# Where the rows of the output projection are kept, and when they are fetched, in a hybrid decoder layer

## The chip, the core and the metric

The kernel runs on one core of a Trainium2 chip. The core has a matrix engine (PE, with its weight loads shown as PEld), three engines for element-wise work (DVE, ACT, POOL), a queue (SP) from which the DMA transfers are issued, and 16 DMA engines that carry them out. Matmul results go to PSUM, eight banks of 128 partitions by 512 words; everything else that is worked on lies in SBUF. The metric is the device time of one execution in microseconds (us), lower being better.

## What is computed

One decoder layer over 1024 tokens of width 1024, in float32:

```
h = rmsnorm(x, mix_pre_norm);  z = h @ w_in
a = mla(...)                         # latent attention, 8 heads
c = short_gated_conv(...)
m = concat(rmsnorm(a), rmsnorm(c))
x = x + rmsnorm(m @ w_out, mix_post_norm)
h = rmsnorm(x, ffn_pre_norm)
f = (silu(h @ w_gate) * (h @ w_up)) @ w_down
x = x + rmsnorm(f, ffn_post_norm)
e = rmsnorm(p @ w_ple_proj, ple_norm)
return x + sigmoid(x @ w_ple_gate) * e
```

The change lies between the attention and the FFN: in the product with w_out, the residual sum, the norm before the FFN and the turn of its result for the FFN.

## The kernel before

**Precision.** Every float32 operand is split into a high and a low part (`split`, L208 to L215: ACT makes the high part, DVE the low one), and every product is three matmuls (`mm3`, L217 to L223: high x high, high x low, low x high).

**Memory.** SBUF is shared out by hand. The arena `mem_r` holds split operands, `mem_f` float32 values: 30 units of 512 words on each partition. An arena call `mf(n, where)` takes n neighbouring units within the ranges of `where`; of the free ones it takes those that have been free longest, and with n = 2 and a range it steps by 2. "Free" is meant in the order in which the program is written. At run time an instruction that writes a place waits until the earlier readers and writers of that place are done, the DMA transfers among them. PSUM banks are given out in turn by `ps.get`.

**Order.** Each engine, and SP, works through its own list in order. The lists are made from the order of the program text by a scheduler, which may put an instruction ahead of others on the same engine; so the order in a trace isn't always that of the text.

**The stage.** The output projection runs over T = 8 tiles of 128 tokens. Its half over the convolution's channels, `wo_c`, runs early, beside the attention, and leaves its rows in `y_d` in DRAM. The other half runs in the loop at L1261, `for t in range(T + 2)`. For a tile t these steps follow each other, each one turn of the loop or more after the one before:

- `load_y(t)` (L1056) fetches the row y of tile t from y_d, 128 x 1024 words, two units.
- `wo_a(t)` (L1071): 24 matmuls (L221 to L223) into two PSUM banks, then DVE adds them to y (L1074) and so empties the banks; then the mean square on ACT (L231) and its root on POOL (L228).
- `load_x(t)` (L1060) fetches the row of the residual stream; `wo_x1(t)` (L1078) norms y, adds that row (L1080, L1082, on DVE) and stores the sum to x1_d (L1084); then the next mean square.
- `wo_n(t)` (L1089) writes the normed row into the place of the x row (L1092) and frees y.
- `h2_turn(t)` (L1103) transposes that row on PE (L1113), copies it out of PSUM and splits it. For the first four tiles the copy goes to a place `raw` (L1108, L1115), from which it is stored to `hr_d` (L1123). For the last four it goes straight into `tr[0]` and `tr[1]` (L1117), four units each, which become the FFN's blocks B12 and B22.

Turn t of the loop runs wo_a(t), wo_x1(t-1), load_x(t), wo_n(t-2), h2_turn(t-3) and, at its end, load_y(t+1) for t from 1 to 6; load_y(0) and load_y(1) stand ahead of the loop. The rows y, the rows x and raw are taken from the range `ML`, units 0 to 21. Of these the gains g_mix and g_ffn hold 18 to 21 until the end of the loop, and the weights of the FFN's first pair of blocks, raw_load(0, 0), hold four of units 0 to 7. tr[0] holds units 22 to 25 and tr[1] units 26 to 29 from before the loop.

**Behind it.** After the eighth wo_a come the first products of the FFN (`product`, L1199 to L1202), whose weights are fetched by raw_load (L1155); raw_load(1, 0) and raw_load(0, 1) take places in units 0 to 17 at t = 8 and t = 9. The FFN uses a scheme with seven products for eight (p = 1 to 7); the blocks for the others are sums and differences made on DVE (L1315) and split (L210, L211). hr_d is read back at t = 9.

Of the kernel before, what the change touches and what calls it, by code (L numbers as in the profile page):

```python
# [45 lines left out]
T = S // P  # L46
# [53 lines left out]
def free(*bufs):  # L100
    for b in bufs:
        m = b.arena
        m.clock += 1
        for i in range(b.lo, b.lo + b.n):
            assert m.live[i]
            m.live[i] = False
            m.freed[i] = m.clock
# [28 lines left out]
def hybrid_layer(ctx: ExitStack, tc: tile.TileContext, x, x_t, p_t, cols_in, positions,  # L136
# [16 lines left out]
    mf = Arena(big.tile([P, FU * U], F32, name="mem_f"), FU)  # L153
# [19 lines left out]
    RR = ((64, 72), (16, 24))  # L173
    RG = ((56, 72),)
    BJ = ((32, 64),)
    ML, MG, MW = ((0, 22),), ((18, 22),), ((0, 8),)


    zeros = cp.tile([P, U // 2], mybir.dt.bfloat16, name="zeros")
# [27 lines left out]
    def split(h, l, src, gain=None, eng=None):  # L207

        if gain is None:
            act.copy(h, src)  # L210
            (eng or dve).tensor_tensor(l, src, h.bitcast(F32), op=ALU.subtract)  # L211
        else:
            act.mul(h, src, gain)
            dve.scalar_tensor_tensor(l, src, gain, h.bitcast(F32), op0=ALU.mult,
                                     op1=ALU.subtract)  # L215
# [20 lines left out]
    def bank3(ap, k):  # L236
        return ap.rearrange("p (k c) -> p k c", k=k)
# [330 lines left out]
    for step in START.split():  # L568
        op, t = step[0], int(step[1:] or 0)
# [484 lines left out]
    rows_y, rows_x = {}, {}  # L1054

    def load_y(t):  # L1056
        rows_y[t] = mf(2, ML)
        sp.dma_start(rows_y[t].a, y_d[t * P : (t + 1) * P, :])

    def load_x(t):  # L1060
        rows_x[t] = mf(2, ML)
        sp.dma_start(rows_x[t].a, x[t * P : (t + 1) * P, :])

    def row_norm(t, i):
# [6 lines left out]
    def wo_a(t):  # L1071
        y = rows_y[t].a
        ids, b = wo_half(t, mTa, 0)
        dve.scalar_tensor_tensor(y, b, ss_a[:, t : t + 1], y, op0=ALU.mult, op1=ALU.add)  # L1074
        ps.put(ids)
        row_norm(t, 0)

    def wo_x1(t):  # L1078
        y, xr = rows_y[t].a, rows_x.pop(t)
        dve.scalar_tensor_tensor(y, y, ss_y[:, 2 * t : 2 * t + 1], g_mix.a, op0=ALU.mult,  # L1080
                                 op1=ALU.mult)
        dve.tensor_tensor(y, y, xr.a, op=ALU.add)  # L1082
        rows_n[t] = xr
        sp.dma_start(x1_d[t * P : (t + 1) * P, :], y)  # L1084
        row_norm(t, 1)
# [3 lines left out]
    def wo_n(t):  # L1089

        y = rows_y.pop(t)
        dve.scalar_tensor_tensor(rows_n[t].a, y.a, ss_y[:, 2 * t + 1 : 2 * t + 2], g_ffn.a,  # L1092
                                 op0=ALU.mult, op1=ALU.mult)
        free(y)
# [3 lines left out]
    tf, tr = {}, {}  # L1098

    def four(b):  # L1100
        return b.a.rearrange("p (k c) -> p k c", k=4)

    def h2_turn(t):  # L1103
        src = rows_n.pop(t)
        o = slice(t % 4 * P, (t % 4 + 1) * P)
        first = t < T // 2
        if first:
            raw = mf(2, ML)  # L1108
        for q in range(2):
            ids, b = ps.get()  # L1110
            for j in range(4):
                k = 4 * q + j
                pe.transpose(b[:, j * P : (j + 1) * P], src.a[:, k * P : (k + 1) * P], ident[:])  # L1113
            if first:
                act.copy(raw.a[:, q * U : (q + 1) * U], b)  # L1115
            else:
                act.copy(four(tr[q])[:, :, o], bank3(b, 4))  # L1117
            if first or q:
                h, l = tf["B" + "12"[q] + "12"[not first]]
                split(four(h)[:, :, o], four(l)[:, :, o], bank3(b, 4))  # L1120
            ps.put(ids)
        if first:
            sp.dma_start(hr_d[:, :, o], raw.a.rearrange("p (k c) -> p k c", k=KD))  # L1123
            free(raw)
        free(src)
# [12 lines left out]
    def pair(n, where):  # L1138
        return mr(n, where), mr(n, where)
# [11 lines left out]
    def raw_load(fp, i, where=None):  # L1151

        for m, w in enumerate((w_gate, w_up)):
            raws[fp, m, i] = r = mf(2, where)
            sp.dma_start(r.a, w[2 * fp + i])  # L1155

    def factor(fp, m, p):
        eng = pool if fp else dve
        a = raws[fp, m, 0].a
        a11, a12 = a[:, 0:U], a[:, U:]  # L1160
        if p == 1:
            src = a11
        elif p == 2:
            src = a12
        else:
            b = raws[fp, m, 1].a
            a21, a22 = b[:, 0:U], b[:, U:]
            if p == 6:
                eng.tensor_tensor(a21, a21, a22, op=ALU.add)
                eng.tensor_tensor(a11, a21, a11, op=ALU.subtract)  # L1170
                src = a11
            elif p == 5:
                src = a21
            elif p == 7:
                eng.tensor_tensor(a21, a22, a11, op=ALU.subtract)
                src = a21
            elif p == 3:
                eng.tensor_tensor(a12, a12, a11, op=ALU.subtract)
                src = a12
            else:  # L1180
                src = a22
        h, l = wp[fp, m, p] = pair(1, RR)
        split(h.a, l.a, src)
        if p == ORDER[-1]:
            free(raws.pop((fp, m, 0)), raws.pop((fp, m, 1)))
# [3 lines left out]
    def product(fp, m, p):  # L1189
        key = fp, m, {1: "X", 6: "X", 7: "X", 4: "X", 2: "Z", 5: "Y", 3: "Y"}[p]  # L1190
        if key not in bank:
            bank[key] = ps.get()
        ids, b = bank[key]
        wh, wl = wp.pop((fp, m, p))
        th, tl = (four(v) for v in tf[RIGHT[p]])
        first, last = p in (1, 2, 5), p in (2, 3, 4)
        for k in range(4):
            c = slice(k * P, (k + 1) * P)
            pe.matmul(b, wh.a[:, c], th[:, k], start=first and k == 0, stop=False,  # L1199
                      skip_group_check=True)  # L1200
            pe.matmul(b, wh.a[:, c], tl[:, k], start=False, stop=False, skip_group_check=True)  # L1201
            pe.matmul(b, wl.a[:, c], th[:, k], start=False, stop=k == 3, skip_group_check=True)  # L1202
        free(wh, wl)

        c = {1: "11", 2: "11", 6: "12", 3: "12", 5: "22", 7: "22", 4: "21"}[p]
        if p in (1, 6, 5, 4):
            blk[fp, m, c] = mf(1, ((0, 18), (22, 30)) if fp < 3 else None)
        o = blk[fp, m, c].a
        g = blk[fp, 0, c].a
        if p in (1, 6, 5):  # L1210
            act.copy(o, b)
        elif p == 4 and m == 0:
            act.activation(o, b, AF.Silu)
        elif p == 4:
            dve.tensor_tensor(o, b, g, op=ALU.mult)
        else:
            dve.tensor_tensor(o, b, o, op=ALU.add)  # L1217
            if m == 0:
                act.activation(o, o, AF.Silu)
            else:  # L1220
                dve.tensor_tensor(o, o, g, op=ALU.mult)
        if last:
            ps.put(ids)
            del bank[key]
# [30 lines left out]

    load_y(0)
    load_y(1)
    raw_load(0, 0, MW)
    tr[0], tr[1] = mf(4, ((22, 26),)), mf(4, ((26, 30),))
    head = [(0, m, p) for p in (1, 2) for m in range(2)]  # L1260
    for t in range(T + 2):  # L1261
        if t < T:
            wo_a(t)
        elif t == T:
            for d in (mTa, wo):
                for h, l in d.values():
                    free(h, l)
            for i in head[:2]:
                product(*i)
        elif t == T + 1:  # L1270
            for i in head[2:]:
                product(*i)
        if 1 <= t <= T:
            wo_x1(t - 1)
        if t == T:
            free(g_mix)
        if t < T:
            load_x(t)
        if 2 <= t <= T + 1:
            wo_n(t - 2)  # L1280
        if t == T + 1:
            free(g_ffn)
            tf["T1"], tf["T4"] = pair(4, BT), pair(4, BT)
            b11, b21 = tf["T1"][1].a.bitcast(F32), tf["T4"][1].a.bitcast(F32)
            sp.dma_start(b11.rearrange("p (k c) -> p k c", k=4), hr_d[:, 0:4, :])
            sp.dma_start(b21.rearrange("p (k c) -> p k c", k=4), hr_d[:, 4:8, :])
        if t >= 3:
            h2_turn(t - 3)
        if 1 <= t < T - 1:
            load_y(t + 1)  # L1290
        if t == T + 1:
            raw_load(0, 1, ((0, 18),))
        if t == T:
            raw_load(1, 0, ((0, 18),))
            for m in range(2):
                raws[2, m, 0] = r = mr(2, BT)
                r.a = r.a.bitcast(F32)
                sp.dma_start(r.a, g2_d[m])
        if t == T // 2:
            for i in head:  # L1300
                factor(*i)
# [246 lines left out]
    for i in range(n2):  # L1548
# [17 lines left out]
        if j in tail:  # L1566
            f, t = tail[j]
# [66 lines left out]
```

## Time and profile before

| | us |
|---|---|
| time, median of 3 runs | 1227.46 (1225.0 to 1229.59) |
| the profiled execution, its own time | 1224.95 |
| its span in the trace | 1223.2 |
| PE busy | 1199.8 (98% of the span) |
| DVE busy | 816.7 (67%) |
| ACT busy | 589.0 (48%) |
| POOL busy | 507.8 (42%) |
| mean granted clock of PE | 0.994 |

The times of single instructions below all come from the one profiled execution. A busy PE isn't PE at its peak, since matmuls overlap in the pipeline: a matmul that is listed with 0.39 us may follow the one before after 0.23. What a stage loses is read from the distance between the starts of its matmuls. In lines of the timeline the first number is the start in us from the beginning of the span, the second the time taken, and the bracket at the end gives the idle time of the engine just before, and what ended it. The page's chain follows the last instruction back to what released it, step by step.

### The profile page before, as it was taken

The page shows a single profiled execution, that of the slowest core. Times are in us where ns is not written, and L with a number is a line of the kernel's source. Part 1 is how long each engine was busy: PE and PEld are TensorE (multiplying, and loading weights), DVE is VectorE, ACT ScalarE, POOL GpSimd, SP SyncE. Part 2 cuts the span into 40 slices and gives each one's busy share as a digit, 9 for nine tenths or more (in the row PEclk, how much of TensorE's full clock was granted, in tenths as well). Part 3 has the DMA queues.
Part 4 walks back from the last instruction along what each step waited for, and adds up shares of the span by engine and source line. Part 5 has one row for each costly group of instructions (what it writes and reads, how often), then busy time and mean ns, then how long its engine had stood idle before and what let it go on. Part 6 is the DMA issues. An engine that isn't in the chain of part 4 may idle for free.

```text
span 1223.2 us, 16697 instructions
## 1 busy us (share of the span) xinstructions
PE 1199.8 (98%) x5918; PEld 1011.3 (83%) x5918; DVE 816.7 (67%) x1173; ACT 589.0 (48%) x1079; POOL 507.8 (42%) x392
## 2 busy tenths in 40 slices
PE   8999999999999998999999999999999999999998
PEld 6998888889999887777888888888888888888886
DVE  6666346478866756896866556565658577758775
ACT  7543333267767734653343333333335556545552
POOL 4433434226654311109888646765724012203321
PEclk8999999999999999999999999999999999999999
DMA  8712563994561667724665336534566576664431
GB/s 300 265 35 94 182 216 125 282 367 86 135 161 53 220 206 237 267 75 184 207 231 193 131 117 207 181 139 144 207 199 198 191 225 236 198 205 159 138 129 70
DMA packets 90174, 219.88 MB, mean 180 GB/s; under 512 B 9094, under 2 KB 18090, under 8 KB 88746
## 3 DMA queue, kind: packets, MB, share of 16 engines
q1 hardware_dynamic: 89744, 218.27, 53.8%
q8 instruction: 46, 0.75, 0.3%
q10 hardware_dynamic: 346, 0.54, 0.2%
q14 instruction: 38, 0.31, 0.1%
HBM read 147.47 MB, written 72.09 MB: 180 GB/s over the span
## 4 chain that ended last, share of the span: by engine, by line
PE 84%; DVE 6%; DMA 5%; ACT 2%; issue 2%; POOL 1%; SPq 0%; DVEq 0%; POOLq 0%; ACTq 0%
PE banks L1202 10%; PE banks L1201 10%; PE banks L1199 10%; PE banks L221 8%; PE banks L223 8%; PE banks L222 8%; PE banks L1407 6%; PE banks L1405 6%; PE banks L1406 6%; DVE mem_r L211 3%; PE banks L895 2%; PE banks L1517 1%; PE banks L1516 1%; PE banks L1514 1%; PE banks L866 1%
## 5 line engine op out<-in xcount | busy, mean ns | idle before, releaser
L211 DVE TENSOR_TENSOR mem_r<-mem_f,mem_r 128x512 fp32r<-128x512 f32 (+1 forms) x400 | 378.3, 977 | 195.8 <-ACT mem_r L210 184.9
L210 ACT CAST mem_r<-mem_f 128x512 fp32r<-128x512 f32 (+2 forms) x403 | 256.6, 666 | 398.3 <-PE banks L1201 129.7
L1199 PE MATMUL banks<-mem_r 128*128 128x512 f32 x616 | 240.4, 391 | 2.8 <-ACT mem_f L1117 2.1
L1202 PE MATMUL banks<-mem_r 128*128 128x512 f32 x616 | 239.9, 391 | 3.1 <-DVE mem_r L211 3.1
L1201 PE MATMUL banks<-mem_r 128*128 128x512 f32 x616 | 240.3, 390 | 0.8 <-DVE mem_r L211 0.8
L221 PE MATMUL banks<-mem_r 128*128 128x512 f32 (+2 forms) x536 | 196.5, 373 | 6.4 <-DVE mem_f L1074 3.8
L222 PE MATMUL banks<-mem_r 128*128 128x512 f32 (+2 forms) x536 | 196.9, 369 | 1.2 <-POOL mem_r L211 1.2
L223 PE MATMUL banks<-mem_r 128*128 128x512 f32 (+2 forms) x536 | 196.2, 369 | 0.0
L1202 PEld LDWEIGHTS banks<-mem_r 128*128 128x128 f32 x616 | 116.0, 188 | 28.2 <-DVE mem_r L211 4.3
L1199 PEld LDWEIGHTS banks<-mem_r 128*128 128x128 f32 x616 | 115.8, 188 | 28.0 <-ACT mem_f L1117 2.4
L1201 PEld LDWEIGHTS banks<-mem_r 128*128 128x128 f32 x616 | 116.0, 188 | 25.5 <-DVE mem_r L211 1.2
L221 PEld LDWEIGHTS banks<-mem_r 128*128 128x128 f32 x536 | 101.3, 191 | 23.8 <-DVE mem_f L1074 4.4
L1406 PE MATMUL banks<-mem_r 128*128 128x512 f32 x308 | 119.9, 389 | 0.0
L1407 PE MATMUL banks<-mem_r 128*128 128x512 f32 x308 | 119.8, 389 | 0.0
L1405 PE MATMUL banks<-mem_r 128*128 128x512 f32 x308 | 119.8, 390 | 0.0
L222 PEld LDWEIGHTS banks<-mem_r 128*128 128x128 f32 x536 | 102.2, 191 | 17.2 <-POOL mem_r L211 1.4
L223 PEld LDWEIGHTS banks<-mem_r 128*128 128x128 f32 x536 | 102.0, 190 | 16.4
L880 POOL TENSOR_TENSOR mem_f<-mem_f,stats 128x640 f32<-128x640 f32 (+5 forms) x64 | 73.4, 1160 | 92.0 <-DVE stats L879 49.7
L228 POOL TENSOR_TENSOR small<-small,mhalf 128x1 f32<-128x1 f32 (+2 forms) x46 | 37.8, 824 | 172.7 <-DVE small L227 172.6
L1217 DVE TENSOR_TENSOR mem_f<-banks,mem_f 128x512 f32<-128x512 f32 x66 | 45.3, 686 | 56.7 <-PE banks L1202 55.6
L211 DVE TENSOR_TENSOR mem_r<-banks,mem_r 128x512 fp32r<-128x512 f32 (+3 forms) x118 | 69.2, 611 | 15.8 <-ACT mem_r L210 15.2
L1406 PEld LDWEIGHTS banks<-mem_r 128*128 128x128 f32 x308 | 57.8, 188 | 12.1 <-DVE mem_r L211 0.2
(199 smaller groups left out, 1896.4 us busy)
## 6 DMA issues: line engine op xcount, KB each, us to landing
sc_d<-mem_f SPq DMA_DIRECT2D x77, 256.0 KB, 2.9
mem_f<-sc_d SPq DMA_DIRECT2D x77, 256.0 KB, 3.0
mem_f<-in_w_gate_dram SPq DMA_DIRECT2D x22, 512.0 KB, 5.1
mem_f<-in_w_up_dram SPq DMA_DIRECT2D x22, 512.0 KB, 4.2
mem_f<-in_w_down_dram SPq DMA_DIRECT2D x22, 512.0 KB, 4.4
wc_d<-mem_f SPq DMA_DIRECT2D x22, 512.0 KB, 3.0
mem_f<-wc_d SPq DMA_DIRECT2D x44, 256.0 KB, 3.6
mem_f<-in_w_down_dram SPq DMA_DIRECT2D x33, 256.0 KB, 3.6
```

The source lines that it names most:

```text
L210: act.copy(h, src)
L211: (eng or dve).tensor_tensor(l, src, h.bitcast(F32), op=ALU.subtract)
L221: pe.matmul(o, wh, vh, start=i == 0, stop=False)
L222: pe.matmul(o, wh, vl, start=False, stop=False)
L223: pe.matmul(o, wl, vh, start=False, stop=i == n - 1)
L880: pool.tensor_tensor(pt.a[:, 0:n], pt.a[:, 0:n], sm.to_broadcast([P, n]), op=ALU.mult)
L1199: pe.matmul(b, wh.a[:, c], th[:, k], start=first and k == 0, stop=False, skip_group_check=True)
L1201: pe.matmul(b, wh.a[:, c], tl[:, k], start=False, stop=False, skip_group_check=True)
L1202: pe.matmul(b, wl.a[:, c], th[:, k], start=False, stop=k == 3, skip_group_check=True)
L1405: pe.matmul(b, ah.a[:, c], bh.a, start=first, stop=False, skip_group_check=True)
L1406: pe.matmul(b, ah.a[:, c], bl.a, start=False, stop=False, skip_group_check=True)
L1407: pe.matmul(b, al.a[:, c], bh.a, start=False, stop=last, skip_group_check=True)
```

## The change

A new range `MX`, units 22 to 29, which are the later places of tr[0] and tr[1], serves the rows y of tiles 0 to 3, the row x of tile 3 and raw of h2_turn. `ML` becomes units 0 to 17 and serves the other rows. tr[0] and tr[1] are taken at the top of turn t = T - 1 = 7 instead of ahead of the loop. load_y(t + 2) is called at the top of turn t, for t from 0 to 5, in place of load_y(t + 1) at the end of turn t.

```diff
-    ML, MG, MW = ((0, 22),), ((18, 22),), ((0, 8),)
+    ML, MX, MG, MW = ((0, 18),), ((22, 30),), ((18, 22),), ((0, 8),)
...
     def load_y(t):
-        rows_y[t] = mf(2, ML)
+        rows_y[t] = mf(2, MX if t < 4 else ML)
         sp.dma_start(rows_y[t].a, y_d[t * P : (t + 1) * P, :])

     def load_x(t):
-        rows_x[t] = mf(2, ML)
+        rows_x[t] = mf(2, MX if t == 3 else ML)
         sp.dma_start(rows_x[t].a, x[t * P : (t + 1) * P, :])
...
         first = t < T // 2
         if first:
-            raw = mf(2, ML)
+            raw = mf(2, MX)
...
     raw_load(0, 0, MW)
-    tr[0], tr[1] = mf(4, ((22, 26),)), mf(4, ((26, 30),))
     head = [(0, m, p) for p in (1, 2) for m in range(2)]
     for t in range(T + 2):
+        if t == T - 1:
+            tr[0], tr[1] = mf(4, ((22, 26),)), mf(4, ((26, 30),))
+        if t < T - 2:
+            load_y(t + 2)
         if t < T:
             wo_a(t)
...
         if t >= 3:
             h2_turn(t - 3)
-        if 1 <= t < T - 1:
-            load_y(t + 1)
```

## The prediction

> **What bounds the kernel now.** The page first: the span, and the chain that ended last by engine.
>
> ```profile
> span 1223.2 us, 16697 instructions
> PE 84%; DVE 6%; DMA 5%; ACT 2%; issue 2%; POOL 1%; SPq 0%; DVEq 0%; POOLq 0%; ACTq 0%
> ```
>
> The matmuls set the time: the chain is 84% PE. The change moves loads, so it can only remove time in which PE stood still or ran slowly. Where that is, the view of PE's waits tells, asked for the stage that the change touches and the stretch behind it (437 to 546 us; columns: total us, times, longest):
>
> ```profile
> PE banks L221 <- DVE mem_f L1074: 3.8, 2, 3.3
> PE banks L1199 <- ACT mem_f L1117: 2.1, 1, 2.1
> PE banks L1202 <- DVE mem_r L211: 1.6, 1, 1.6
> PE banks L1201 <- DVE mem_r L211: 0.8, 1, 0.8
> PE banks L1199 <- DVE small L227: 0.6, 1, 0.6
> ```
>
> L221 is a matmul of the output projection, which waits for PSUM banks that L1074 (in wo_a) must empty. Why L1074 is late, the waits of DVE and of SP's queue say:
>
> ```profile
> DVE mem_f L1074 <- DMA mem_f<-y_d: 4.7, 3, 3.6
> SPq L1058 <- DMA hr_d<-mem_f: 11.5, 4, 4.5
> ```
>
> L1074 waits for a row that load_y (L1058) fetches, and that fetch waits four times for a store to hr_d. The code agrees, if the allocator's rule (of the free places, the one free longest) is followed by hand. Nine places of two units lie below the gains; two hold the first weights. The rows y0, y1, x0, x1, y2, x2, y3 fill the seven others. From then on each row takes a place just left: x3 that of y0, raw of tile 0 (L1108) that of y1, and y4 raw's, so that the store from raw (L1123) must land first. y5, y6 and y7 stand to raw of tiles 1, 2 and 3 in the same way. The timeline shows what it costs (start, us, what; in brackets the idle time before):
>
> ```profile
> 464.09 0.58 SPq L1123 DMA_DIRECT2D hr_d<-mem_f  x1
> 470.63 0.33 SPq L1058 DMA_DIRECT2D mem_f<-y_d  x1
> 475.77 1.28 DVE L1074 SCALAR_TENSOR_TENSOR mem_f<-banks,small,mem_f 128x1024 f32<-128x1024 f32 x1 [3.61 <-DMA mem_f<-y_d]
> 477.11 0.74 PE L221 MATMUL banks<-mem_r 128*128 128x512 f32 x1 [3.28 <-DVE mem_f L1074]
> ...
> 480.87 0.39 PE L221 MATMUL banks<-mem_r 128*128 128x512 f32 x1
> 481.10 0.40 PE L222 MATMUL banks<-mem_r 128*128 128x512 f32 x1
> ...
> 484.08 0.39 PE L223 MATMUL banks<-mem_r 128*128 128x512 f32 x1
> 484.96 0.50 PE L221 MATMUL banks<-mem_r 128*128 128x512 f32 x1 [0.49 <-DVE mem_f L1074]
> 485.30 0.40 PE L222 MATMUL banks<-mem_r 128*128 128x512 f32 x1
> ```
>
> Row 4's load is issued at 470.63, when tile 0's store has landed; L1074 starts at 475.77, PE goes on at 477.11. A matmul is due every 0.23 us (480.87 to 481.10), but the nine from 477.11 to 480.87 take 3.76: the clock had dropped.
>
> **The change part by part.** No instruction is added or removed; all 16 row loads stay, at some 0.33 us of SP each.
>
> *Places.* Rows 0 to 3, row 3 of x and raw (L1108) move to the 8 units that tr[0] and tr[1] held from the start; tr is first written by h2_turn(4), and is now claimed at t = 7. The seven other places are left to y4 to y7 and to seven rows of x. By the same rule x0, x1, y4, x2, y5, y6 and x4 each get one that nothing in this stage has used; y7 gets that of x0, x5 that of x1, x6 that of x2 (each free after that tile's transposes), x7 that of y4. None of the y waits for hr_d. At the end the second pair's weights (raw_load(1, 0)) get the places of x4 and y6, as before.
>
> *Order.* load_y(t+2) at the top of turn t passes on SP the load of x (L1062) and the stores L1084 and L1123 of turns t and t+1. Row 4's fetch can go with row 1 or 2 of x, some 20 us before use:
>
> ```profile
> 445.86 0.33 SPq L1062 DMA_DIRECT2D mem_f<-in_x_dram  x1
> ```
>
> As no slot is waited for, nothing on SP queues behind them. The DMA engines have room there:
>
> ```profile
> 438.00:472.20 34.20, 34.20 (x163) 28.50 (x162) 26.14 (x34) 15.06 (x28) 6.95 (x9) 1.00 0.54 185
> 472.20:490.60 18.40, 14.64 (x64) 11.60 (x63) 11.12 (x14) 8.61 (x16) 1.62 (x3) 0.91 0.71 240
> 490.60:516.40 25.80, 23.05 (x109) 18.69 (x108) 19.77 (x28) 16.10 (x29) 3.59 (x5) 0.93 0.87 312
> 516.40:546.00 29.60, 27.21 (x118) 21.62 (x117) 29.60 (x29) 18.61 (x25) 0.00 (x0) 1.00 0.12 39
> ```
>
> (Columns: stretch, length, then busy time of PE, PEld, DVE, ACT, POOL, granted clock, DMA share, GB/s.) Four rows of 512 KB over the first stretch add 2.1 MB / 34.2 us = 61 GB/s to 185: cost nothing, where the third stretch moves 312. They leave the two later, fuller ones.
>
> *What goes.* (a) The stall, 3.28 us. (b) Its cold clock: 3.76 - 9 x 0.23 = 1.7. (c) Row 5's stall: 484.08 to 485.30 is 1.22, less 2 x 0.23: 0.8. (d) Row 7's:
>
> ```profile
> 492.56 0.32 SPq L1058 DMA_DIRECT2D mem_f<-y_d  x1
> 496.16 1.28 DVE L1074 SCALAR_TENSOR_TENSOR mem_f<-banks,small,mem_f 128x1024 f32<-128x1024 f32 x1 [0.51 <-DMA mem_f<-y_d]
> 497.59 0.47 PE L1199 MATMUL banks<-mem_r 128*128 128x512 f32 x1 [0.56 <-DVE small L227]
> ```
>
> 0.6, as L1074 of tile 7 held the banks. Together 6.4 us.
>
> A rule of the Trainium skill is weighed here: "TensorE: Matmul & The Clock Gate", section "What's actually happening", has PE fall to half rate only after an idle window of about 3.4 us. By it neither that stall nor the one of 2.11 us below would have cost any clock; the PE terms would be 4.7 to 6.8 us and the forecast, in their middle, some 5.8 below the median, 1221.7, within 0.5%. The rows above show the slow matmuls after 3.28 us, and those below after 2.11, so the measurement decides: (b) stays, and that result gets no chance of its own.
>
> *What is late next.* (e), the product behind the head of the FFN:
>
> ```profile
> 493.88 9.64 DMA mem_f<-in_w_gate_dram
> 503.55 1.14 ACT mem_r L210 x2
> ...
> 506.63 0.48 ACT mem_f L1117
> ```
>
> ```profile
> 507.15 0.50 PE L1199 MATMUL banks<-mem_r 128*128 128x512 f32 x1 [2.11 <-ACT mem_f L1117]
> ...
> 511.60 0.40 PE L1199 MATMUL banks<-mem_r 128*128 128x512 f32 x1
> ```
>
> PE waits 2.11 us for a bank that ACT (L1117) empties late, as ACT had waited for a weight row; then the clock is low again (twelve matmuls up to 511.60 in 4.45 us, 2.76 due: 1.7 us). The weight's load was issued at 493.88, behind row 7's, which had blocked SP until 492.56 for the store of tile 3. That block goes, and the stretch's DMA gets lighter by that row; but the load still starts only when tile 4's transposes free its place, right after the last wo_a, and PE arrives 0.6 us sooner. So (e) is worth between 0 and 3.8 us. All PE terms: 6.4 to 10.2.
>
> *What DVE allows.* Behind the stage DVE is the bound: 29.60 of 29.60 us busy from 516.4 to 546, and PE waits for it there (L1202, L1201 above, 1.6 and 0.8). So PE keeps only what DVE gains before 516.4. DVE does 11.12 + 19.77 = 30.9 us of work in the 44.2 from 472.2. Where rows came in time it was busier:
>
> ```profile
> 452.00:462.00 10.00, 10.00 (x48) 8.30 (x47) 9.46 (x11) 3.12 (x7) 2.56 (x3) 1.00 0.40 151
> 462.00:472.00 10.00, 10.00 (x53) 8.39 (x51) 7.86 (x12) 6.69 (x14) 1.63 (x3) 1.00 0.78 247
> ```
>
> 17.3 of 20 us, 87%. At that pace 30.9 us take 35.7, so DVE allows 8.5 us. I take 7.5, midway between the 6.4 that PE surely has and these 8.5.
>
> *New waits, which the trace can't show.* First, raw of tile 1 gets raw of tile 0's place, so its copy (L1115, ACT) waits for that store, as row 4 did before: issued 464.09, landed by 470.6 at the latest. In this trace the copy waited 1.2 us for the store of the row whose place it had:
>
> ```profile
> 463.35 0.60 ACT L1115 COPY mem_f<-banks 128x512 f32<-128x512 f32 x1
> 469.34 0.59 ACT L1115 COPY mem_f<-banks 128x512 f32<-128x512 f32 x1 [1.20 <-DMA x_d<-mem_f]
> ```
>
> So between a gain of 1.2 and a loss of 1.3 us on ACT; behind it stand the casts and row 4's norm (L231), and PE asks only for L1074, which comes before them: taken as 0, the middle. Second, L1117 of tile 4, the first to write tr, waits for the store of tile 3:
>
> ```profile
> 475.03 6.90 DMA hr_d<-mem_f
> ...
> 488.99 3.49 DMA hr_d<-mem_f
> ```
>
> ```profile
> 491.17 1.08 ACT L1117 COPY mem_f<-banks 128x512 f32<-128x512 f32 x2 [0.67 <-PE banks L1113]
> ```
>
> That store landed at 492.5, 1.3 us after the copy's time; with the longest landing, 6.9, it would be 4.7. Behind L1117 stand tile 7's norms; PE has four products of 12 x 0.23 = 2.8 us, 11 us in all, as cover. Taken as 0; without that cover 1.3 to 4.7; a gain is excluded, since the copy waited for no store before.
>
> **The sum.** The profiled execution took 1224.95 us, 1.75 around its span. Less 7.5: 1217.5. It lay 2.5 below the median of 1227.46, from which the forecast is counted: 1220.0. About 0.5%, 6.1 us, can be told from no change: 1221.3 is the border.
>
> **The rivals.** *Forecast, 0.50:* row stalls gone, DVE follows, gain 6.4 to 8.5: 1219.0 to 1221.1.
>
> *The late bank goes too, 0.12:* the weight lands sooner since SP is free and DMA lighter; gain 10.2: 1217.3. For it speaks the blocked SP; against it DVE's 8.5.
>
> *DVE takes the place, 0.20:* only its waits for rows go (4.7 us); the waits on POOL and ACT of each tile's chain stay, and the packed 29.6 us start 4.7 earlier: 1222.8. For it speaks that packed stretch; against it the 87% with rows in time.
>
> *The store finds another victim, 0.12:* one of the two new waits reaches PE through ACT's queue (4.7 plus 1.7 of cold clock taken from 6.4 leaves 0), or the new order of the queues undoes the early loads, so that the change doesn't do what it says: 1227.5, or 1225 with half.
>
> *Slower, 0.06:* the stores to hr_d are issued late on SP. The longest wait of L1123 on SP is 6.6:
>
> ```profile
> SPq L1123 <- ACT mem_r L210: 8.7, 4, 6.6
> ```
>
> With 6.9 to land, tile 1's copy comes up to 13.5 us after 463.8, at 477.3 instead of 469.3; DVE's splits of that tile wait for it and, if they stand before L1074 of tile 5, PE too: 8.0 + 1.7 = 9.7 us. It decides once the copies lose over 6.4 us on PE's path; at one place the kernel ends 3.3 slower, 1230.8, at both (tiles 1 and 4) 13.0 slower, 1240.5. Against it: after 438 SP is mostly idle.
>
> **How the numbers follow.** Faster by over 0.5%: the first two cases, less the part of the forecast near the border, 0.58. Within 0.5%: DVE, another victim, and that part, 0.36. Slower: 0.06. The range goes from 1216 (all PE terms, and a median low by 1.3) to 1225.5 (half of the victim case); it leaves out the slower case, the rest of the victim case and the outer edges.
>
> **What the profile will show.** Rows 4 to 7 issued before 475, and L1058 without a wait for hr_d; no wait of L1074 on y_d; L221 without a stall, and the clock at 1.00 from 472 to 490. The last wo_a ends some 5.8 us earlier, at 484 to 485. DVE's packed stretch starts at about 509 instead of 516.4. The forecast is wrong if that stretch starts less than 5 us earlier, if L1115 or L1117 waits for hr_d for over 5 us, or if the rows are still issued late.

## The result, and the profile after

| | before | after |
|---|---|---|
| time, median (lowest to highest, runs), us | 1227.28 (1225.0 to 1229.59, 4) | 1213.95 (1213.01 to 1215.04, 4) |
| the profiled execution, us | 1224.95 | 1213.01 |
| its span, us | 1223.2 | 1211.0 |

The ratio is 0.9903, 95% interval 0.9885 to 0.992 (the two medians alone give 0.9891): the changed kernel is faster by 13.3 us, about 1%. The forecast was a gain of 7.5 us, and the time lies below the range. In the profiled executions the gain is 11.9 us (span 12.2); the other 1.4 are scatter between executions, and what follows is about the 12.

From the page of the kernel after, the span, and the chain that ended last by engine:

```profile
span 1211.0 us, 16715 instructions
...
PE 92%; DMA 2%; DVE 2%; ACT 2%; issue 1%; POOL 1%; SPq 0%; ACTq 0%; DVEq 0%; POOLq 0%
```

The chain is PE now by 92%, against 84%: its steps through DMA went from 5% to 2%, through DVE from 6% to 2%. All waits of PE from 437 to 546 us in the kernel after (total us, times, longest):

```profile
PE banks L1113 <- DVE mem_f L1092: 2.5, 1, 2.5
PE banks L1199 <- ACT mem_f L1211: 1.1, 1, 1.1
```

L221 does not wait at all, and the waits for L1117, L211 and L227 are gone. Two are new: the transposes of the last tile (L1113) wait 2.5 us for its normed row, and a product of the FFN waits 1.1 for a copy by ACT (L1211). The busy times in windows of the kernel after (columns as in the prediction):

```profile
438.00:472.20 34.20, 34.20 (x162) 28.52 (x161) 25.44 (x33) 14.61 (x28) 6.90 (x9) 1.00 0.67 223
472.20:490.60 18.40, 18.40 (x95) 15.52 (x94) 17.30 (x23) 11.35 (x23) 4.75 (x6) 1.00 0.83 281
472.20:504.34 32.14, 29.69 (x149) 24.90 (x148) 28.01 (x38) 22.33 (x43) 6.20 (x8) 0.95 0.88 318
504.34:534.00 29.66, 28.54 (x126) 23.29 (x125) 29.66 (x32) 18.74 (x26) 0.00 (x0) 1.00 0.12 43
```

From 472.2 to 490.6 PE is busy all the time at a clock of 1.00 (before: 14.64 of 18.40, at 0.91). The stretch in which DVE has no gap is there as before, 29.66 of 29.66 us, counted here from the first sum of the FFN's blocks, which starts at 504.34, where it had started at 516.45. (A few short instructions without a gap stand just ahead of it; with them the stretch starts at 501.93 and 514.64.) That sum, before and after, from the timeline of DVE:

```profile
516.45 2.28 DVE L1315 TENSOR_TENSOR mem_f<-mem_f 128x2048 f32<-128x2048 f32 x1
```

```profile
504.34 2.29 DVE L1316 TENSOR_TENSOR mem_f<-mem_f 128x2048 f32<-128x2048 f32 x1
```

To compare executions, the path of PE is cut into four pieces, from the timeline's matmuls: the stage (from the first matmul of L221 after L805, at 438.06 and 438.01 us, to the last of the output projection), the FFN's products up to the last L1202, the down projection, and the last loop. "Lost" is the sum, over the FFN's matmuls, of the distance between starts beyond 0.229 us for each (0.098 for a transpose): stalls together with the slow matmuls behind them, good to some tenths as a few records are missing. "Last turn" and "first sum" are starts counted from the start of the stage.

| profiled execution | stage | last turn | first sum | FFN | lost in it: up to the first sum, behind | down | last loop | all four |
|---|---|---|---|---|---|---|---|---|
| before | 52.6 | 76.3 | 78.4 | 433.1 | 5.4, 5.4 | 211.3 | 83.0 | 780.1 |
| after | 46.7 | 62.7 | 66.3 | 428.3 | 4.7, 1.4 | 211.5 | 81.5 | 768.0 |
| difference | -5.9 | -13.6 | -12.1 | -4.8 | -0.7, -4.0 | 0.2 | -1.5 | -12.1 |

So the stage gave what it was forecast to give. (Its length before is not the same in every execution: in three others with the old places it is 51.3, 51.4 and 52.7.) What was not forecast is 4 us behind the first sum, in products whose code the change does not touch, and 1.5 in the last loop.

### The profile page after: what moved, and what is told of

Read it like the earlier page. It is cut to its first block, busy times and chain, and to the rows that moved or that the text cites. A ratio compares the mean times of both kernels' runs of the same rounds, so it can differ in the third digit from the quotient of the medians.

```text
span 1211.0 us, 16715 instructions
## 1 busy us (share of the span) xinstructions
PE 1195.7 (99%) x5918; PEld 1010.6 (83%) x5918; DVE 810.8 (67%) x1173; ACT 588.4 (49%) x1079; POOL 504.9 (42%) x392
## 4 chain that ended last, share of the span: by engine, by line
PE 92%; DMA 2%; DVE 2%; ACT 2%; issue 1%; POOL 1%; SPq 0%; ACTq 0%; DVEq 0%; POOLq 0%
PE banks L1199 11%; PE banks L1201 11%; PE banks L1202 11%; PE banks L221 8%; PE banks L223 8%; PE banks L222 8%; PE banks L1407 6%; PE banks L1408 6%; PE banks L1406 6%; PE banks L895 2%; PE banks L1518 2%; PE banks L1517 2%; PE banks L1515 2%; PE banks L866 1%; PE banks L923 1%; PE banks L925 1%
## 5 line engine op out<-in xcount | busy, mean ns | idle before, releaser
L211 DVE TENSOR_TENSOR mem_r<-mem_f,mem_r 128x512 fp32r<-128x512 f32 (+1 forms) x400 | 372.5, 963 | 195.6 <-ACT mem_r L210 185.7
L210 ACT CAST mem_r<-mem_f 128x512 fp32r<-128x512 f32 (+1 forms) x403 | 256.7, 667 | 392.6 <-PE banks L1201 131.0
L1202 PE MATMUL banks<-mem_r 128*128 128x512 f32 x616 | 239.0, 389 | 0.0
L221 PE MATMUL banks<-mem_r 128*128 128x512 f32 (+2 forms) x536 | 195.6, 372 | 2.4 <-ACT mem_r L210 1.5
L1202 PEld LDWEIGHTS banks<-mem_r 128*128 128x128 f32 x616 | 115.7, 188 | 24.0
L221 PEld LDWEIGHTS banks<-mem_r 128*128 128x128 f32 x536 | 101.0, 190 | 18.9 <-ACT mem_r L210 2.1
L211 DVE TENSOR_TENSOR mem_r<-banks,mem_r 128x512 fp32r<-128x512 f32 (+3 forms) x118 | 69.3, 613 | 15.8 <-ACT mem_r L210 15.2
```

What stands on the lines that cost most here:

```text
L221: pe.matmul(o, wh, vh, start=i == 0, stop=False)
```

## The experiments

Times are medians, each with its ratio to runs of the kernel before made beside it. The median of these runs went from 1224.99 to 1227.41 us, so times from different sections are comparable to about 2 us only, and the ratios better. The losses come from one profiled execution each, which is not always near the median: that of places alone lies 3.4 us above its median, that of the kernel before with the turn ahead 4.3 above, that of the kernel after with the turn behind 2.6 below. The theory at the start was: the stage's gain comes from the store to hr_d alone; the rest comes of DVE, which is bound behind the stage and so pays every microsecond that it gets ahead. The rival: it comes of the order in which PE's work is listed.

**Raw alone, and the places without the early loads.** The first is the kernel before with two edits (and the definition of MX), the second the kernel after with load_y(t + 1) back at the end of the turn:

```diff
-            raw = mf(2, ML)
+            raw = mf(2, MX)
...
-    tr[0], tr[1] = mf(4, ((22, 26),)), mf(4, ((26, 30),))
     for t in range(T + 2):
+        if t == T - 1:
+            tr[0], tr[1] = mf(4, ((22, 26),)), mf(4, ((26, 30),))
```

> Only raw of h2_turn moves to the units of tr, and tr is taken at t = 7; the rows y and x stay in units 0 to 17 and y is fetched one tile ahead as before. Theory A (the stores to hr_d held the places of rows 4 to 7, and nothing else was wrong): no fetch of y waits for hr_d; row 4 comes in time, so the 3.3 us stall of PE and its cold clock go (5 us); rows 5 to 7 now take the place that wo_n leaves one turn before, so a small stall at row 7 (up to 2.5 us) may stay. The last wo_a ends 4 to 6 us earlier than before, the whole 6 to 11 us: 1216 to 1221. Rival (the lead of two tiles is what counts, not who holds the place): rows 4 to 7 are still late, gain under 3 us, over 1224.

> All places as in the changed kernel, but y fetched at the end of the turn, one tile ahead, as before. Theory A (places): rows 4 to 6 have places that nothing holds, so their fetches are issued early all the same; within 1.5 us of the changed kernel, 1212.5 to 1215.5. Rival (lead): it loses what the lead gives, 3 us or more, over 1217.

Raw alone: 1218.96 us, ratio 0.9937 (0.9916 to 0.9957). Places alone: 1219.34, 0.9941 (0.9924 to 0.9959). In both the stage takes 46.7 us, as in the kernel after. So the stage's gain is the store to hr_d that a row no longer waits for, and moving raw is enough for it; fetching rows ahead adds nothing there. The rest of the gain is not had with either, so that for places alone the rival's number came (over 1217), not the theory's. Raw alone loses 10.3 us in the FFN, 7.6 of it behind 510; places alone loses 13.0, and its last turn waits longer for row 7 than that of the kernel after. (The row's load is issued at the same time, 48.1 us from the stage's start against 48.0, but DVE has the row later.)

```profile
502.86 1.97 PE L1113 MATMUL banks<-ident,mem_f 128*128 128x128 f32 x8 [4.05 <-DVE mem_f L1092]
```

**More work for DVE.** To the kernel after, two more sums of 128x2048, ahead of the four that it has:

```diff
+    for _ in range(2):
+        t_sum(t2.a, b22.a, b12.a, ALU.subtract)
```

> The changed kernel with two more sums of 128x2048 on DVE (2.3 us each, 4.6 in all) right after the last h2_turn, ahead of the FFN's first sum. Their result is overwritten, nothing else changes. Theory A (in the FFN's first 60 us PE waited for a DVE that came 8 us too late, and the change helped by letting DVE come earlier): the waits of PE for DVE's splits that the changed kernel no longer has come back, 2 to 4.6 us in all: 1216 to 1218.5. Rival B (those waits went because the scheduler put the lists in another order): no wait comes back, 1213 to 1215.

1221.43 us, 0.9955 (0.9941 to 0.997): 7.5 more than the kernel after, for 2 x 2.28 = 4.6 us of work, and more than the 1216 to 1218.5 that was expected. It appears as waits of PE for splits, 5.6 us in all; the longest, from the timeline of PE:

```profile
532.45 1.22 PE L1199 MATMUL banks<-mem_r 128*128 128x512 f32 x2 [4.00 <-ACT mem_r L210]
```

So in that stretch DVE's chain has little slack, and more than its own length is lost when it is late. That fits the first theory, but also any theory in which this chain starts late.

**Row 7 of x earlier.** In the kernel after its load waits for the place of y4. Here y4 goes to MX, row 3 of x to ML, and load_y(t + 2) stands behind the claim of the x row, so that row 7 gets a place free long before:

```diff
-        rows_y[t] = mf(2, MX if t < 4 else ML)
+        rows_y[t] = mf(2, MX if t < 5 else ML)
...
-        rows_x[t] = mf(2, MX if t == 3 else ML)
+        rows_x[t] = mf(2, ML)
...
```

> The changed kernel, but y of tile 4 also lies in the units of tr, x of tile 3 in the others, and load_y(t + 2) stands behind wo_n(t - 2). So x of tile 7 gets the place of x of tile 3 (free after its transposes, about 479) and no longer that of y of tile 4 (free after wo_n, 485). Theory: in the changed kernel the last turn of h2 waits 2.45 us on PE because x of tile 7 is fetched at 486 and lands at 496; with the fetch at 480 that stall and its cold clock (some 1.9 us) go: 1209.5 to 1212. Rival: the stall moves to the next late thing (the weights of the second pair, or DVE's own work, 17.3 of 18.4 us busy), gain under 1 us: 1213 to 1214.5.

1212.97 us, 0.9889 (0.9867 to 0.9911), short of the 1209.5 to 1212 that was expected. The load is issued at 481.52 - 440.25 = 41.3 us from the stage's start instead of 486.05 - 438.01 = 48.0, and the wait at the last turn falls to 0.39:

```profile
500.88 1.26 PE L1113 MATMUL banks<-ident,mem_f 128*128 128x128 f32 x8 [0.39 <-DVE mem_f L1092]
```

The FFN loses 3.2 us instead of 6.1 and takes 425.3 instead of 428.3. The last loop takes 82.8 instead of 81.5, so that little is left; the interval overlaps that of the kernel after.

**Less work for DVE.** If DVE's load were the bound, taking work off it should pay. First the sums of the weight blocks (L1169 to L1178), of which DVE does a part, all go to POOL, in the kernel before, the kernel after, and the one with the early row:

```diff
-        eng = pool if fp else dve
+        eng = pool
```

> The kernel before, with the seven small sums of the FFN's first pair that factor makes on DVE (L1169 to L1178, 0.68 us each) moved to POOL, which does nothing from 512 to 542. Theory A (PE waits for a DVE that is packed from 516 to 546): DVE has 4.8 us less there, PE's waits on L211 behind 516 (3.9 us in all in the kernel before) shrink by 2 us or more; 1222 to 1225.5. Rival B (those waits hang on the order of the lists or on POOL, not on DVE's load): no gain, or a loss where POOL's sums, twice as long, come late: 1226.5 to 1231.

> The changed kernel with the same seven sums on POOL. Theory A: DVE's packed stretch already comes early enough, PE has one wait of 1.1 us left behind 516; so the same edit is worth less than 1.2 us here: 1212.5 to 1215. If the edit is worth as much here as in the kernel before, DVE's lead wasn't what the change gave.

> The version with x of tile 7 fetched early (e4) with the same seven sums on POOL. Theory A: both remaining waits are touched; 1211 to 1213.5, the best so far or equal to e4. Rival: POOL's longer sums come late and PE waits for them: over 1214.

1228.15 (1.0025, 1.0011 to 1.004), 1218.03 (0.9942, 0.9927 to 0.9957) and 1219.4 (0.9952, 0.9936 to 0.9967): all slower than the kernel that they are made from. Then, in the kernels before and after, the four large sums are left out, and the splits read the blocks as they are:

```diff
     def t_sum(o, x, y, op):
-        dve.tensor_tensor(o, x, y, op=op)
+        pass
...
-    t_split("T2", t2.a)
+    t_split("T2", b12.a)
...
```

(The split of T4 reads b22 in the same way, which is freed later for it.)

> The kernel before without the FFN's four sums of 128x2048 on DVE (L1315, 2.28 us each, 9.1 in all); the blocks are split from B12 and B22 as they are, so these sums are left out of the computation. Theory A (PE waits in the FFN's first 60 us for the chain last turn of h2, first sum, second sum, split of T2 on DVE): T2 is ready 5 to 9 us sooner, PE's waits for L211 behind 516 (3.9 us with those at 568 and 592) go, nothing else; 1222.5 to 1225.5. Rival B (the order of the lists): no such gain, within 1.5 us of before.

> The changed kernel without the same four sums. Theory A: T2 is already early there (split at 517.6, used at about 528), so the same 9.1 us of DVE work are worth at most the one wait of 1.1 us that is left: 1212 to 1214.5. Rival B: worth as much here as in the kernel before.

1231.86 (1.0046, 1.0032 to 1.0061) and 1223.73 (0.9988, 0.9976 to 1.0001): with 9.1 us less work on DVE the kernels are 6 and some 10 us slower than theirs. These five missed. The traces show two things that can account for it, which these runs do not separate. One is in the lists: with the sums gone, large splits come ahead of small ones that PE needs. The timeline of DVE in the kernel after without the sums, and the wait on PE's:

```profile
506.93 6.68 DVE L211 TENSOR_TENSOR mem_r<-mem_f,mem_r 128x2048 fp32r<-128x2048 f32 x2
```

```profile
519.23 0.80 PE L1202 MATMUL banks<-mem_r 128*128 128x512 f32 x1 [3.42 <-DVE mem_r L211]
```

The other is that POOL and DVE hinder one another; it is shown in the last section. It is at work here too: one such split takes 2.28 us at 530.94 in the same trace, with POOL idle, where the two above take 6.68 beside POOL's sums. In the three runs with the sums on POOL there is a plainer cause besides: a sum of 128x512 takes 1.6 us there, 0.68 on DVE. What these runs settle is that the amount of DVE's work does not say by itself when PE gets its operand. They don't test the load alone, since the order moved with it.

**The order of the last turn.** In the kernel before the last tile's transposes stand behind two products on PE (pair 1, p = 1), in the kernel after ahead of them. From the timelines of PE, before and then after:

```profile
514.37 1.03 PE L1113 MATMUL banks<-ident,mem_f 128*128 128x128 f32 x8
```

```profile
500.69 1.97 PE L1113 MATMUL banks<-ident,mem_f 128*128 128x128 f32 x8 [2.45 <-DVE mem_f L1092]
502.47 0.79 PE L1199 MATMUL banks<-mem_r 128*128 128x512 f32 x1
503.06 0.63 PE L1201 MATMUL banks<-mem_r 128*128 128x512 f32 x1
...
504.47 0.40 PE L1199 MATMUL banks<-mem_r 128*128 128x512 f32 x1
```

The text of the program has not changed at this place; the order that the scheduler made of it has. The turns of tiles 4 to 6 have moved among the first four products too: before, those of tiles 5 and 6 stand together behind all four, 48 matmuls behind tile 4's; after, tile 5's stands nine behind tile 4's. The next two kernels move the last turn alone, back in the kernel after, and ahead in the kernel before; a third is the one with the early row, with the last loop's order written out.

```diff
-    h2_turn(T - 1)
+    with tc.issue_after(tail_mm[0].ins):
+        h2_turn(T - 1)
```

(tail_mm[0] is the last matmul of these two products; the second kernel sets the products behind the last transpose in the same way.)

> The changed kernel with its last turn (the eight transposes of tile 7) queued behind the two products (1, m, 1) instead of ahead of them. Theory 'cover': the chain from the last turn to the split of T2 on DVE takes about 19 us (18.8 before, 19.2 after), and PE has eight products, 21.8 us, before it needs T2 when the turn stands ahead, six, 16.4, when it stands behind. So the stall of 2.45 us at the turn and its cold clock go (worth 2.9 us where x7 was loaded early), and waits for L211 or L210 of 2 to 5 us come back between 515 and 545: FFN 427.4 to 430.4 us, time 1213 to 1216. Rival 'no matter': the order of the turn is worth nothing, only the stall counts: FFN 425.4, time 1211, and no wait over 1 us behind 515.

> The kernel before, with its last turn queued ahead of the two products (1, m, 1), everything else as it was. Theory 'cover': the waits for L211 behind 529 (1.6, 0.8, 1.1 us) go, but the turn now stands where PE reaches it some 5 us earlier, while row 7 of x and the late weight row come as they did, so PE stalls there by 3 to 6 us instead of 2.1: time 1226 to 1231. Rival 'order alone': the order of the turn, not the rows' places, made the gain behind the stage: FFN 4 to 5 us shorter, time 1222 to 1223.

The kernel after with the turn behind: 1221.99 us, 0.9965 (0.9953 to 0.9976), 8 more than the kernel after. Its stage (46.7) and last loop (81.6) are those of the kernel after; its FFN takes 434.1, 5.9 more. The two longest waits, the turn between them and the wait that follows, from the timeline of PE, and the first sum from that of DVE:

```profile
502.69 0.80 PE L1200 MATMUL banks<-mem_r 128*128 128x512 f32 x1 [3.75 <-ACT mem_r L210]
512.77 1.03 PE L1113 MATMUL banks<-ident,mem_f 128*128 128x128 f32 x8
529.30 0.69 PE L1200 MATMUL banks<-mem_r 128*128 128x512 f32 x1 [1.87 <-ACT mem_r L210]
530.25 0.80 PE L1202 MATMUL banks<-mem_r 128*128 128x512 f32 x1 [0.27 <-DVE mem_r L211]
```

```profile
514.90 2.29 DVE L1317 TENSOR_TENSOR mem_f<-mem_f 128x2048 f32<-128x2048 f32 x1 [0.77 <-ACT mem_f L1117]
```

The direction was expected, the size was not: 4.8 us more are lost behind the first sum, as the waits for splits come back there, and the two products, now first, wait 3.75 for a split of their own, a time that the turn had filled. Some of the size may be the edit's: in the trace 38 matmuls stand between the last two turns, where the kernel before had 24. But raw alone has 24 there and its rows in time, and loses 7.6 behind 510 as well. The first sum waits for the copy of the turn (L1117): it needs B12 and B22 whole.

The kernel before with the turn ahead: 1229.18 us, 1.0025 (1.001 to 1.0039), no gain, as expected. Only one product still stands ahead of the turn, but the row came no sooner. The timelines of DVE have the last normed row, before and in this kernel:

```profile
510.46 1.28 DVE L1092 SCALAR_TENSOR_TENSOR mem_f<-mem_f,small 128x1024 f32<-128x1024 f32 x1 [0.66 <-POOL small L228]
```

```profile
512.17 1.28 DVE L1092 SCALAR_TENSOR_TENSOR mem_f<-mem_f,small 128x1024 f32<-128x1024 f32 x1 [0.66 <-POOL small L228]
```

That is 72.4 and 72.6 us from the stage's start, and the last turn starts at 76.3 and 76.1. On its way PE now waits longer for the late bank, the product behind it runs at the low clock (0.50 granted from 510.33 to 515.6), and then comes the turn:

```profile
510.33 0.79 PE L1200 MATMUL banks<-mem_r 128*128 128x512 f32 x1 [3.73 <-ACT mem_f L1118]
515.62 1.14 PE L1114 MATMUL banks<-ident,mem_f 128*128 128x128 f32 x8
```

So rows in time with the turn behind (raw alone, which has 24 matmuls ahead of it, and the kernel after with the turn behind) and an earlier turn without rows in time lose most or all of what the kernel after gains in the FFN. Both are needed.

| profiled execution | stage | last turn | first sum | FFN | lost in it | last loop |
|---|---|---|---|---|---|---|
| kernel before, turn ahead | 52.7 | 76.1 | 77.9 | 436.5 | 14.3 | 86.2 |
| after, turn behind | 46.7 | 74.1 | 76.2 | 434.1 | 11.9 | 81.6 |
| raw alone | 46.7 | 67.0 | 71.7 | 432.6 | 10.3 | 84.0 |
| places alone | 46.7 | 64.3 | 67.9 | 435.2 | 13.0 | 84.2 |
| after | 46.7 | 62.7 | 66.3 | 428.3 | 6.1 | 81.5 |
| after, row 7 early | 46.7 | 60.6 | 64.3 | 425.3 | 3.2 | 82.8 |

The FFN less what it loses is 422.1 to 422.3 in every row, so the differences lie in these losses alone. The first sum follows 1.8 to 4.7 us behind the last turn each time. Places alone is the row that the time of the turn doesn't explain. From the first sum to 580 it has a single wait, of 1.11, as the kernel after has one of 1.12; but 4.3 of its losses lie from 580 to 600, where the kernel after has none, behind a wait of 2.03 for a split, although its products have the same list as those of the kernel after. Why that split is late is not settled; the execution is the slowest of its six, so the others may not have this wait.

**The last loop.** In the list of the kernel after, two turns of the last loop stand together, 16 transposes in a row, and PE has no wait there; before, there was one:

```profile
1163.46 0.50 PE L1517 MATMUL banks<-mem_r 128*128 128x512 f32 x1 [1.15 <-DVE mem_r L211]
```

The kernel with the early row has the older list, and 0.90 of wait. So the two turns were set ahead in it:

> The kernel with x7 in an early place (1212.97), with the turns of tiles 2 and 3 put ahead of the third product of the last loop and the matmuls held behind them, so that the tail's list is like that of the changed kernel. Theory 'tail list': the tail falls from 82.8 to about 81.4 us, time 1211.6. Rival: the difference between the tails is not of the list but of what comes before it, tail 82.8 as it was, time 1213.0.

1212.85 us, 0.9889 (0.9865 to 0.9913), a last loop of 83.1: no gain. The old wait is gone, another has come in its place:

```profile
1147.64 0.50 PE L1516 MATMUL banks<-mem_r 128*128 128x512 f32 x1 [1.16 <-DVE mem_f L1530]
```

The order that was written out is not that of the kernel after, only nearer to it. That 1.5 us of the gain come from the reordered list of the last loop is therefore argued, not shown: the five kernels with that list (after, more for DVE, after with POOL, after without the sums, turn behind) have 81.5 to 82.2 and at most 0.38 of wait, eight others with the older one 82.8 to 86.2 and a wait of 0.9 to 2.5. Neither of the two kernels at 1213 is told apart from the kernel after by its interval.

## Why the prediction was wrong, point by point

**(a) to (c), the stage: right.** 3.28, 1.7 and 0.8, together 5.8 us; measured 5.9 in the profiled executions. The signs named came as well: all eight loads of y were issued by 462.6, L1074 does not wait for y_d, the clock stayed at 1.00. The timeline of SP in the kernel after:

```profile
423.76 0.33 SPq L1058 DMA_DIRECT2D mem_f<-y_d  x1
...
426.16 3.02 SPq L1058 DMA_DIRECT2D mem_f<-y_d  x3
...
439.21 0.32 SPq L1058 DMA_DIRECT2D mem_f<-y_d  x1
...
441.97 5.27 SPq L1058 DMA_DIRECT2D mem_f<-y_d  x2
...
462.54 0.32 SPq L1058 DMA_DIRECT2D mem_f<-y_d  x1
...
486.05 0.71 SPq L1062 DMA_DIRECT2D mem_f<-in_x_dram  x1
```

Raw alone shows that the place of raw did it, and the rest of the places and the early loads were not needed for it.

**(d) and (e): inside their bounds, by another way.** They were put at 0.6 to 4.4 together; up to the first sum the FFN loses 0.7 less. The wait (d) is gone, and (e) gave nothing on balance: the wait of 2.11 for L1117 is gone too, but at 500.69 the last turn waits 2.45 for row 7 of x, whose load (486.05 above) had to wait until y4's place was free, as the prediction had found for that place without asking what it costs. From the timeline of DVE:

```profile
496.10 1.23 DVE L1082 TENSOR_TENSOR mem_f<-mem_f 128x1024 f32<-128x1024 f32 x1 [1.51 <-DMA mem_f<-in_x_dram]
499.35 1.28 DVE L1092 SCALAR_TENSOR_TENSOR mem_f<-mem_f,small 128x1024 f32<-128x1024 f32 x1
```

With that row early, the loss up to the first sum is 1.8.

**The two new waits: right to cost nothing.** L1115 of tile 1 did wait for the store, and nothing on PE waited for it; L1117 did not wait:

```profile
469.90 0.59 ACT L1115 COPY mem_f<-banks 128x512 f32<-128x512 f32 x1 [1.84 <-DMA hr_d<-mem_f]
```

**The step that failed: "So PE keeps only what DVE gains before 516.4."** With it the sum was cut to 7.5, and nothing behind 516 was entered as a gain. Up to the first sum PE gained 5.9 + 0.7 = 6.6 us, close to the 6.4 that the prediction was sure of; behind it came 4.0 us that the sum had put at nothing. The pace that the step assumed was found: 28.01 of 32.14 us from 472.2 to the first sum are 87%. By that pace alone, with the same work ahead of it, the first sum would have come 8.5 us earlier; it came 12.1 earlier, with 28.0 us of DVE's work ahead of it instead of 30.9. What had changed is the order: the sum needs the last turn, and in every run that has the sum it follows within 5 us. (A wait of DVE for the turn's copy shows only where the turn was put behind, 0.77 above; elsewhere the sum stands in DVE's list behind short work.) Before, the turn stood behind two products of 12 matmuls each, 24 x 0.229 = 5.5 us, and behind the stage's stalls; after, it came 13.6 us earlier, 7.7 more than the stage gained. What makes the scheduler put it ahead is not shown: it does so in places alone, not in raw alone, and in both the stage takes 46.7, its rows in time.

And a packed DVE is not yet a bound for PE. All waits of PE up to 620, before from 512 on, then after from 504 on:

```profile
PE banks L1202 <- DVE mem_r L211: 3.1, 3, 1.6
PE banks L1201 <- DVE mem_r L211: 0.8, 1, 0.8
```

```profile
PE banks L1199 <- ACT mem_f L1211: 1.1, 1, 1.1
```

The stretch is as packed as before, yet PE no longer waits for DVE in it; its one wait is for ACT. Of the four waits before, the prediction had seen the first two (1.55 and 0.77) and read them as DVE's limit; the other two (1.12 and 0.44) lie behind the stretch that it looked at. That they went, with the slow matmuls behind them, and that the one for ACT came, is the 4.0 us. With the turn behind, in otherwise the same kernel, 4.8 come back.

**The last loop: not in the sum at all.** 1.5 us, with the reservation above.

**The rivals.** The late bank as it was priced (1217.3) named a wait that did go, but the wait for row 7 took its place; DVE taking the place (1222.8), another victim and the slower case did not come. Missing was the rival that a planner that orders the lists anew moves work that the change does not touch.

## What to carry to other kernels

An engine that is busy without a gap is a bound only as long as its output comes after it is wanted: before you cap a gain by it, find the instruction that opens its packed stretch, and what that one waits for. Where lists are made by a scheduler, moving a load can reorder work far from it, for better or worse by as much as the load itself is worth (here 4.0 of FFN beside 5.9 of the stage), so that the order of both kernels has to be compared before their times are. And of several moves in a change, one can carry its main part alone: try them singly.

## What the hardware showed that was not expected

POOL and DVE slow one another when both read SBUF. The sum of 128x2048 takes 2.28 us on DVE with POOL idle. With the weights' sums on POOL in the kernel before, the timeline of all engines has:

```profile
512.93 1.63 POOL L1178 TENSOR_TENSOR mem_f<-mem_f 128x512 f32<-128x512 f32 x1
513.48 3.23 DVE L1315 TENSOR_TENSOR mem_f<-mem_f 128x2048 f32<-128x2048 f32 x1
514.52 3.35 POOL L1169 TENSOR_TENSOR mem_f<-mem_f 128x512 f32<-128x512 f32 x1
516.63 0.68 DVE L211 TENSOR_TENSOR mem_r<-banks,mem_r 128x512 fp32r<-128x512 f32 x1
```

DVE's sum takes 3.23: POOL's ends at 514.56, 1.08 behind its start, and 1.08 + 2.28 = 3.36 is near the time found. POOL's next one, begun at 514.52, takes 3.35 instead of some 1.6; DVE's sum ends 2.19 behind its start, so that in the same way it would be 3.8. The split that reads one operand from PSUM (banks) keeps its 0.68. The Trainium skill, "SBUF — State Buffer", section "SBUF: two separate sides", says that the two share a port pair which one instruction holds to its end while the other blocks, for DVE operations with two inputs in SBUF, against an operation of POOL that reads SBUF; DVE's row agrees to 0.13 us, POOL's only roughly. So work that is moved from DVE to POOL can come back as waiting on both.

The clock dropped again after short idle times: in the kernel after, behind the wait of 2.45, the granted clock is 0.50 from 500.69 to 502.47, and the two steps from 502.47 to 503.49 are 0.59 and 0.43 us where 0.23 are due. The length of the wait alone doesn't decide it: behind the wait of 2.03 in places alone the clock is 0.56 from 589.9 to 593.6, but behind one of 2.02 in the kernel before with the turn ahead, at 523.82, it stays at 1.00. So two stalls of one length can cost differently.
